# Values on all rows with column halves in turn, scores grouped over row strips, and an output projection that goes token by token: one change to a Trainium2 kernel on one core

## The chip, the cores and the metric

One core of a Trainium2 chip. The metric is the device time of one launch in microseconds; 1990.25 is the median of three runs before the change. Everything is computed in fp32.

## The reference

A hybrid network for 512 tokens of width 1024. Two layers, each: RMS norm, one wide input projection, and from its parts three mixers whose outputs are joined, projected and added to x; then a feed-forward part (norm, up, causal convolution over three tokens, silu gate, down). After a norm, a second block with windowed, grouped-query and cross attention, three gated branches, an output projection with its own norm, and a residual addition. The parts that matter here:

```python
def gla_chunked(q, k, v, log_a):            # 4 heads, keys 32 wide, values 64 wide, chunks of 64 tokens
    ...
        b = jnp.cumsum(gb, axis=-2)
        inter = jnp.einsum('bhik,bhkv->bhiv', qb * jnp.exp(b), state)
        ...
        A = jnp.einsum('bhik,bhjk,bhijk->bhij', qb, kb, dec)
        intra = jnp.einsum('bhij,bhjv->bhiv', A, vb)

def retention_chunked(q, k, v):             # 4 heads of the same sizes, a fixed decay for each head
    ...
    scores = jnp.einsum('bhnid,bhnjd->bhnij', qc, kc) * D[None, :, None]
    intra = jnp.einsum('bhnij,bhnjv->bhniv', scores, vc)
    U = jnp.einsum('bhnjd,bhnjv->nbhdv', k_dec, vc)

# the end of the second block
    merged = gates[:, :, 0] * ya + gates[:, :, 1] * yb + gates[:, :, 2] * ym
    out = merged @ w_out[layer]
    x = x + rms_norm(out, g_post[layer])
```

## The kernel before

**Layout.** x stands in SBUF as eight tiles of 128 channels by 512 tokens (channels on partitions). A dense product in near-fp32 accuracy is three fast matmuls (`mm3`, L442 to 446): both operands are split into a high and a low fp32r part, and high x high, low x high and high x low go into one PSUM bank. `ps` tiles are channel by token (512 tokens moving); `pt` tiles are moved 256 wide. Weights come by DMA in groups (`weight_groups`, L82), three staging buffers, and ACT makes the high and DVE the low part of each (`split_weight`, L411: `whi`, `wlo`; for the output projection `oh`, `ol` in tiles of the general pool).

**Order.** Each engine works in the order in which its instructions stand. Dense projections are generators in a queue (`Fill`, L290). Attention code calls `f(us)` between its small pieces, with a number of the table `PACE` (L28), and the queue then emits dense matmuls worth that time, so that PE has dense work while ACT and DVE prepare the next small piece. `need(name)` empties the queue as far as the named projection.

**The places touched.** `gla` (L774) builds the gated scores by levels: for every level, 32 x 32 to 64 x 64 blocks of decayed keys (`ke`) and queries (`qe`) of four heads are multiplied into four banks `lv`, token tile by token tile, eight instructions (four heads on four 32-row strips, two blocks) and then `f(PACE["gla"])` (L860). DVE copies a level into `gD` under a mask (L871), ACT copies the diagonal blocks from `gD` to `gA` (L875). `states` (L878) makes the chunk states: `U` on PE, then twelve small DVE operations `st`. `mix_out` (L897), which both mixers use, takes two token tiles in one bank `o`: queries times states (L907, `o<-st`), and for each head two value products (L912), one with 64 rows for the first 64 queries, one with 128 rows for the rest; then ACT squares, norm, gate and the transposes `oT`. `ret` (L938) makes its scores head by head: a bank `rsc`, four matmuls on one 32-row strip (L968), DVE's `rA` and dense work. Between `ret`'s scores and its values stands `late()`, the last transposes `yt` of the first mixer (L1056).

PSUM has eight banks: three of tag "d" (`bank`) for dense products and five of tag "m" (`mbank`) in rotation, so that a new tile waits for the readers of the one five before it. `finish` (L1665) does the output projection in two token halves, channel tiles of 128 by 256 tokens; the norm is a sum over channels, which takes PE two small products (`tsq`, `rows`) with DVE's `rsqrt` between, then DVE scales, adds x and SyncE's queue stores; the host transposes the result.

Of the kernel before, what the change touches and what calls it, by code (L numbers as in the profile page):

```python
# [17 lines left out]
S = 512  # L18
# [48 lines left out]
def _span(a, n):  # L67
    return list(range(a, a + n))
# [13 lines left out]
def weight_groups():  # L82
# [69 lines left out]
    two("gm", "w_in_2", k8, _span(GA2 + 1024, 512))  # L152
    branch(1, PAIRED, "w_br_b_2")
    branch(2, k4, "w_br_m_2")
    two("out", "w_out_2", k8, _span(0, 1024))
    return g


# [177 lines left out]
class Prog:  # L336
# [74 lines left out]
    def split_weight(self, i):  # L411
        nc = self.nc
        self.load(i)
        off, k, kt, mc = self.order[i]
        s3 = self.staged.pop(i).rearrange("p (k m) -> p k m", k=kt)
        if i >= self.table[(2, "out", 0)][0]:
            hi, lo = (TileList([self.gt(n, (128, 2, 256), F32R) for _ in range(2)], 2) for n in ("oh", "ol"))
            for j in range(2):
                self.split(hi.tiles[j], lo.tiles[j], s3[:, 2 * j:2 * j + 2])
            self.wt[i] = (k, kt, hi, lo)  # L420
            return
        hi = self.wsp.tile([128, kt, mc], F32R, name="whi", tag="whi")
        lo = self.wsp.tile([128, kt, mc], F32R, name="wlo", tag="wlo")
        nc.scalar.activation(hi, s3, AF.Copy)  # L424
        nc.vector.tensor_sub(lo, s3, hi.bitcast(F32))  # L425
        self.wt[i] = (k, kt, hi, lo)
# [347 lines left out]
    def gla(self, l, bc):  # L774
# [60 lines left out]
        for li, hs in enumerate(seq):  # L835
            qe, ke = nxt
            if li + 1 < len(seq):
                nxt = factors(li + 1, seq[li + 1])
            if li == 1:
                kps = self.mbank("kps")  # L840
                for t in range(3):
                    nc.tensor.transpose(kps[:, T4[t]], kd[:, T4[t]], self.ident)
                kdt = self.gt("kdt")
                nc.scalar.activation(kdt[:, :384], kps[:, :384], AF.Copy)
            if li == 2:
                self.fill.need("gv")
                states = self.states(lambda t: kdt[:, T4[t]], z["gv"], lambda t: eb[:, t * 128 + 127:t * 128 + 128])
            ps = [self.mbank("lv", (128, 4, 64)) for h in range(4)]
            w = hs if hs >= 16 else 64
            step = 2 * hs if hs >= 16 else 64  # L850
            off = hs if hs >= 16 else 0
            for t in range(4):
                for j0 in range(0, 128, step):
                    c0 = (j0 + off) % 64
                    a = t * 128 + j0
                    for h in range(4):
                        hp = slice(32 * h, 32 * h + 32)
                        nc.tensor.matmul(ps[h][j0:j0 + w, t, c0:c0 + w], ke[hp, a:a + w], qe[hp, a + off:a + off + w],  # L858
                                         start=True, stop=True, tile_position=(32 * h, j0))
                f(PACE["gla"])  # L860
            for h in range(4):
                if hs == 64:
                    nc.scalar.activation(A[h][:64, :, 64:], ps[h][:64], AF.Copy)
                elif hs >= 16:
                    for j0 in range(0, 128, step):
                        r, cs = slice(j0, j0 + hs), slice(j0 % 64 + hs, j0 % 64 + 2 * hs)
                        nc.scalar.activation(D[h][r, :, cs], ps[h][r, :, cs], AF.Copy)
                else:
                    mi = MASKED.index(hs)
                    mk = c["gmask"][:, mi * 64:mi * 64 + 64].bitcast(I32)  # L870
                    nc.vector.copy_predicated(D[h], mk[:, None, :].to_broadcast([128, 4, 64]), ps[h])  # L871
            if hs == 0:
                for h in range(4):
                    for r in (slice(0, 64), slice(64, 128)):
                        nc.scalar.activation(A[h][r, :, r], D[h][r], AF.Copy)  # L875
# [21 lines left out]
    def mix_out(self, l, gkey, nkey, A, v, st, qg, bc, b0):  # L897
# [2 lines left out]
        os = []  # L900
        for tp in range(2):
            o = self.mbank("o", (128, 2, 256))
            for j in range(2):
                t = 2 * tp + j
                sl = slice(t * 128, t * 128 + 128)
                if t:
                    nc.tensor.matmul(o[:, j], qg[:, sl], st[t], start=j == 0, stop=True, skip_group_check=True)  # L907
                for h in range(4):
                    hd = slice(64 * h, 64 * h + 64)
                    for n in (64, 128):  # L910
                        r = slice(n - 64, n)
                        nc.tensor.matmul(o[r, j, hd], A[h][:n, t, r], v[t][:n, hd], start=t + h == 0, stop=True,  # L912
                                         skip_group_check=True)
            sq = self.gt("osq")
            nc.scalar.activation(sq, o.rearrange("p t d -> p (t d)"), AF.Square)
            nc.vector.tensor_reduce(v2[:, 8 * tp:8 * tp + 8], sq.rearrange("p (g d) -> p g d", g=8), AX, OP.add)
            os.append(o)
            f(PACE["mix1"])
# [19 lines left out]
    def ret(self, l, bc, late, more):  # L938
# [22 lines left out]
                             c["rqd"][:, None, :].to_broadcast([128, 4, 128]))  # L961
        A = []
        rd = c["rd"].rearrange("p (h i) -> p h i", h=4)
        for h in range(4):
            hp = slice(32 * h, 32 * h + 32)
            ps = self.mbank("rsc", (128, 4, 128))
            for t in range(4):
                nc.tensor.matmul(ps[:, t, :], rk[hp, T4[t]], rq[hp, T4[t]], start=True, stop=True)  # L968
            a = self.gt("rA", (128, 4, 128))
            nc.vector.tensor_mul(a, ps, rd[:, h:h + 1, :].to_broadcast([128, 4, 128]))  # L970
            A.append(a)
            f(PACE["ret2"])
        late()
        for name, g in more:
            self.fill.add(name, g)
# [148 lines left out]
    def run(self):  # L1124
# [9 lines left out]
                if self.stop == (l, "ffn"):  # L1134
                    break
        if self.stop:
            nc.sync.dma_start(self.aps["out"].rearrange("(k p) t -> p k t", p=128), self.x)
            return
        with tc.tile_pool(name="c2", bufs=1) as c2:
            self.cst1 = c2  # L1140
# [2 lines left out]
    def block2(self):  # L1143
# [37 lines left out]
        opm = self.operand("gm", om)  # L1181
        for i in range(4):
            fill.add(("br", 2, i), self.branch(2, i, opm))
        fill.need()
        self.finish()

# [427 lines left out]
    def cross(self):  # L1614
# [47 lines left out]
        self.skew(units, ((0, score), (3, turn), (4, value)), PACE["cross"])  # L1662
        return res

    def finish(self):  # L1665
        nc = self.nc
        for k in range(8):
            self.split(self.xh[:, k], self.xl[:, k], self.merged[k], 0.5)
        kept = {}
        for half in range(2):  # L1670
            tk = slice(256 * half, 256 * half + 256)
            acc = self.gt("acc")[:, :256]
            out = [self.gt("out", (128, 2, 256)) for _ in range(4)]
            for i in range(4):
                if half == 0:
                    kept[i] = list(self.weights((2, "out", i)))
                ps = [self.bank("ps", (128, 256)) for _ in range(2)]
                for k0, kt, hi, lo in kept[i]:
                    for m in range(2):
                        sl = slice(m * 128, m * 128 + 128)  # L1680
                        for k in range(kt):
                            self.mm3(ps[m], hi[:, k, sl], lo[:, k, sl], self.xh[:, k0 + k, tk], self.xl[:, k0 + k, tk],
                                     k0 + k == 0, k0 + k == 7)
                for m in range(2):
                    n = 2 * i + m
                    if n == 0:
                        nc.scalar.activation(acc, ps[m], AF.Square)
                    else:
                        q = self.gt("sq")[:, :256]
                        nc.scalar.activation(q, ps[m], AF.Square)  # L1690
                        nc.vector.tensor_add(acc, acc, q)
                    nc.scalar.activation(out[i][:, m], ps[m], AF.Copy, scale=self.vec("g_post_2", n))
            v = self.tok_sums(acc, 1, 2)
            nc.vector.tensor_scalar(v, v, 1.0 / D, EPS, op0=OP.mult, op1=OP.add)
            r = self.rsqrt(v, "rt", (2, 1))
            R = self.rows(r, 2)[:, :256]
            dst = self.aps["out"].rearrange("(i k p) t -> i p k t", i=4, k=2)
            for i in range(4):
                o = out[i]
                nc.vector.tensor_mul(o, o, R[:, None, :].to_broadcast([128, 2, 256]))  # L1700
                (nc.vector if i else nc.gpsimd).tensor_add(o, o, self.x[:, 2 * i:2 * i + 2, tk])
                nc.sync.dma_start(dst[i][:, :, tk], o)


def arrays_of(inputs):
# [8 lines left out]
    sw = [16 * (d // 16 ^ 1) + d % 16 for d in range(64)]  # L1714
    q, k = inputs["q_norm_2"][0], inputs["k_norm_2"][0]
    a["qkn"] = np.stack([q, q[sw], k, k[sw]])
    a["mla_out"] = np.ascontiguousarray(inputs["mla_out_norm"])
    return a, vec_at, cst_at

# [21 lines left out]
```

## Time and profile before

| | |
|---|---|
| median of three runs | 1990.25 us (1987.42 to 1991.47) |
| profiled execution | 1990.08 us |
| its span | 1988.3 us |
| busy: PE / DVE / ACT / POOL | 98% / 62% / 40% / 7% |
| DMA | 172.30 MB, mean 87 GB/s |

The profile shows one execution. PE is TensorE, DVE VectorE, ACT ScalarE, POOL GpSimd, SP SyncE. Matmuls are pipelined: a dense one shows some 390 ns of duration in the grouped lines (1408 instructions of L444 in 556.8 us), though the next starts earlier; the chain of waits counts from start to start. An fp32 matmul that is not split shows as two records.

### The profile page before, as it was taken

The page shows a single profiled execution, that of the slowest core. Times are in us where ns is not written, and L with a number is a line of the kernel's source. Part 1 is how long each engine was busy: PE and PEld are TensorE (multiplying, and loading weights), DVE is VectorE, ACT ScalarE, POOL GpSimd, SP SyncE. Part 2 cuts the span into 40 slices and gives each one's busy share as a digit, 9 for nine tenths or more (in the row PEclk, how much of TensorE's full clock was granted, in tenths as well). Part 3 has the DMA queues.
Part 4 walks back from the last instruction along what each step waited for, and adds up shares of the span by engine and source line. Part 5 has one row for each costly group of instructions (what it writes and reads, how often), then busy time and mean ns, then how long its engine had stood idle before and what let it go on. Part 6 is the DMA issues. An engine that isn't in the chain of part 4 may idle for free.

```text
span 1988.3 us, 28658 instructions
## 1 busy us (share of the span) xinstructions
PE 1954.8 (98%) x11351; PEld 1620.4 (81%) x11351; DVE 1239.2 (62%) x2299; ACT 793.4 (40%) x1473; POOL 140.7 (7%) x172
## 2 busy tenths in 40 slices
PE   9999999999999999999999999999999999999997
PEld 7879888888888878888888888887888877788887
DVE  6666576646556666576656466845456787655454
ACT  5545243222224635443222224525354456543242
POOL 1000000000000100000000000021131330000000
PEclk9999999999999999999999999999999999999998
DMA  5221123232323321133232334432222221123331
GB/s 196 60 80 44 64 89 101 84 109 85 106 80 107 94 67 50 41 96 95 93 90 96 103 113 123 135 109 67 75 75 67 75 64 54 63 67 98 101 96 54
DMA packets 55189, 172.30 MB, mean 87 GB/s; under 512 B 6494, under 2 KB 10096, under 8 KB 55056
## 3 DMA queue, kind: packets, MB, share of 16 engines
q1 hardware_dynamic: 53152, 165.47, 26.6%
q0 software_dynamic: 1760, 4.87, 0.9%
q8 instruction: 89, 1.46, 0.3%
q14 instruction: 44, 0.36, 0.1%
q10 hardware_dynamic: 144, 0.14, 0.0%
HBM read 167.05 MB, written 2.10 MB: 85 GB/s over the span
## 4 chain that ended last, share of the span: by engine, by line
PE 91%; DVE 5%; ACT 3%; issue 1%; POOL 0%; DMA 0%; DVEq 0%; POOLq 0%; ACTq 0%
PE ps L444 24%; PE ps L446 23%; PE ps L445 23%; PE pt L444 3%; PE pt L445 3%; PE pt L446 3%; PE o L912 2%; DVE wlo L425 1%; PE o L1029 1%; PE s L1006 1%; PE aq L1347 1%; PE bo L1596 1%; PE bpq L1584 1%; PE rows L529 1%; PE lv L858 1%
## 5 line engine op out<-in xcount | busy, mean ns | idle before, releaser
L424 ACT ACTIVATE whi<-wst 128x1024 fp32r<-128x1024 f32 (+3 forms) x318 | 316.3, 995 | 700.3 <-PE ps L445 566.4
L425 DVE TENSOR_TENSOR wlo<-wst,whi 128x1024 fp32r<-128x1024 f32 (+3 forms) x318 | 367.4, 1155 | 315.9 <-ACT whi L424 315.4
L444 PE MATMUL ps<-xh,whi 128*128 128x512 f32 (+1 forms) x1408 | 556.8, 396 | 0.0
L445 PE MATMUL ps<-xl,whi 128*128 128x512 f32 (+1 forms) x1408 | 550.3, 391 | 0.6 <-DVE xl L490 0.6
L446 PE MATMUL ps<-xh,wlo 128*128 128x512 f32 (+1 forms) x1408 | 549.8, 391 | 0.1
L444 PEld LDWEIGHTS ps<-xh,whi 128*128 128x128 f32 (+1 forms) x1408 | 264.4, 188 | 61.1 <-issue 6.7
L446 PEld LDWEIGHTS ps<-xh,wlo 128*128 128x128 f32 (+1 forms) x1408 | 264.3, 188 | 57.1 <-DVE wlo L425 0.9
L445 PEld LDWEIGHTS ps<-xl,whi 128*128 128x128 f32 (+1 forms) x1408 | 264.6, 188 | 55.8 <-DVE xl L490 2.8
L444 PE MATMUL pt<-whi,xh 128*128 128x256 f32 x480 | 143.2, 299 | 1.5 <-ACT bz L1523 0.8
L445 PE MATMUL pt<-wlo,xh 128*128 128x256 f32 x480 | 137.6, 287 | 0.0
L445 PE MATMUL ps<-fl,whi 128*128 128x512 f32 x352 | 137.0, 389 | 0.0
L444 PE MATMUL ps<-fh,whi 128*128 128x512 f32 x352 | 137.0, 389 | 0.0
L446 PE MATMUL ps<-fh,wlo 128*128 128x512 f32 x352 | 136.9, 389 | 0.0
L446 PE MATMUL pt<-whi,xl 128*128 128x256 f32 x480 | 136.5, 286 | 0.0
L444 PEld LDWEIGHTS pt<-whi,xh 128*128 128x128 f32 x480 | 92.7, 194 | 6.7 <-ACT bz L1523 1.3
L1067 DVE TENSOR_TENSOR x<-x,ps 128x512 f32<-128x512 f32 x96 | 65.7, 687 | 50.8 <-PE ps L446 50.6
L445 PEld LDWEIGHTS pt<-wlo,xh 128*128 128x128 f32 x480 | 93.3, 194 | 0.5 <-issue 0.2
L446 PEld LDWEIGHTS pt<-whi,xl 128*128 128x128 f32 x480 | 92.9, 194 | 0.2 <-issue 0.2
L445 PEld LDWEIGHTS ps<-fl,whi 128*128 128x128 f32 x352 | 66.1, 188 | 13.8
L446 PEld LDWEIGHTS ps<-fh,wlo 128*128 128x128 f32 x352 | 66.1, 188 | 13.7
L444 PEld LDWEIGHTS ps<-fh,whi 128*128 128x128 f32 x352 | 66.1, 188 | 13.6
L486 ACT ACTIVATE fh<-cv 128x512 fp32r<-128x512 f32 x44 | 27.9, 633 | 84.7 <-DVE cv L1121 84.7
(464 smaller groups left out, 2919.1 us busy)
## 6 DMA issues: line engine op xcount, KB each, us to landing
wst<-in_w SPq DMA_DIRECT2D x250, 512.0 KB, 3.5
wst<-in_w SPq DMA_DIRECT2D x54, 384.0 KB, 3.0
wst<-in_w SPq DMA_DIRECT2D x20, 256.0 KB, 2.6
x<-in_xT SPq DMA_DIRECT2D x8, 256.0 KB, 4.9
out<-out SPq DMA_DIRECT2D x8, 256.0 KB, 2.3
mt<-in_memT POOLq DMA_DIRECT2D x4, 256.0 KB, 4.1
c<-in_cst POOLq DMA_DIRECT2D x3, 256.0 KB, 3.5
s<-in_cst POOLq DMA_DIRECT2D x3, 256.0 KB, 2.9
```

What stands on the lines that cost most here:

```text
L424: nc.scalar.activation(hi, s3, AF.Copy)
L425: nc.vector.tensor_sub(lo, s3, hi.bitcast(F32))
L444: nc.tensor.matmul(out, lh, rh, start=start, stop=False, skip_group_check=True)
L445: nc.tensor.matmul(out, lh, rl, start=False, stop=False, skip_group_check=True)
L446: nc.tensor.matmul(out, ll, rh, start=False, stop=stop, skip_group_check=True)
L486: nc.scalar.activation(hi, src, AF.Copy)
L529: nc.tensor.matmul(ps[:, t, :], w, self.ident, start=True, stop=True)
L858: nc.tensor.matmul(ps[h][j0:j0 + w, t, c0:c0 + w], ke[hp, a:a + w], qe[hp, a + off:a + off + w], start=True, stop=True, tile_position=(32 ...
L912: nc.tensor.matmul(o[r, j, hd], A[h][:n, t, r], v[t][:n, hd], start=t + h == 0, stop=True, skip_group_check=True)
L1006: nc.tensor.matmul(s[:, :nk], qn[h][:, T4[qt]], kn[h][:, :nk], start=False, stop=True, skip_group_check=True)
L1029: nc.tensor.matmul(O[qt][:, h, :], PT[u][:, T4[kt]], v[kt][:, T4[h]], start=kt == 0, stop=kt == qt)
L1067: nc.vector.tensor_add(xm, xm, ps)
```

## The change

Four edits. In `gla` a level's four token tiles stand in a row, and one pull of four times the pace follows. In `mix_out` the state products of a token pair come first, and every value product uses all 128 rows (the part of `gA` that the mask leaves at zero included), first and second 64 output columns in turn. In `ret` the scores of all heads go to four banks at once, token tile outside and head inside, so that the four 32-row strips take turns, and one pull follows. The output projection keeps tokens on partitions: x is transposed into itself (`residual`, queued between two branches), the split merged activations are the stationary operand, weights move 512 wide in two column groups, the norm is a sum along the free axis (ACT's accumulated square), the gain comes by two broadcasts, and the result is stored without a host transpose.

```diff
@@ weight_groups
-    two("out", "w_out_2", k8, _span(0, 1024))
+    for i in range(2):
+        g.append(((2, "out", i), "w_out_2", 0, k8, _span(512 * i, 512)))
@@ split_weight
-            hi, lo = (TileList([self.gt(n, (128, 2, 256), F32R) for _ in range(2)], 2) for n in ("oh", "ol"))
-            for j in range(2):
-                self.split(hi.tiles[j], lo.tiles[j], s3[:, 2 * j:2 * j + 2])
+            hi, lo = ([self.gt(n, dtype=F32R) for _ in range(kt)] for n in ("oh", "ol"))
+            for j in range(kt):
+                self.split(hi[j], lo[j], s3[:, j])
@@ gla
-                f(PACE["gla"])
+            f(4 * PACE["gla"])
@@ mix_out
             o = self.mbank("o", (128, 2, 256))
+            first = True
             for j in range(2):
                 t = 2 * tp + j
-                sl = slice(t * 128, t * 128 + 128)
                 if t:
-                    nc.tensor.matmul(o[:, j], qg[:, sl], st[t], start=j == 0, stop=True, skip_group_check=True)
+                    nc.tensor.matmul(o[:, j], qg[:, t * 128:t * 128 + 128], st[t], start=first, stop=True,
+                                     skip_group_check=True)
+                    first = False
+            for j in range(2):
+                t = 2 * tp + j
                 for h in range(4):
                     hd = slice(64 * h, 64 * h + 64)
-                    for n in (64, 128):
-                        r = slice(n - 64, n)
-                        nc.tensor.matmul(o[r, j, hd], A[h][:n, t, r], v[t][:n, hd], start=t + h == 0, stop=True,
+                    for r in (slice(0, 64), slice(64, 128)):
+                        nc.tensor.matmul(o[r, j, hd], A[h][:, t, r], v[t][:, hd], start=False, stop=True,
                                          skip_group_check=True)
@@ ret
+        ps = [self.mbank("rsc", (128, 4, 128)) for _ in range(4)]
+        for t in range(4):
+            for h in range(4):
+                hp = slice(32 * h, 32 * h + 32)
+                nc.tensor.matmul(ps[h][:, t, :], rk[hp, T4[t]], rq[hp, T4[t]], start=True, stop=True)
         for h in range(4):
...
-            f(PACE["ret2"])
+        f(4 * PACE["ret2"])
@@ block2
         for i in range(4):
             fill.add(("br", 2, i), self.branch(2, i, opm))
+            if i == 1:
+                fill.add("res", self.residual())
@@ new function
+    def residual(self):
+        nc = self.nc
+        self.xt = self.x.rearrange("p (a b) s -> p a (b s)", b=2).rearrange("p a (t c) -> p a t c", t=4)
+        for kp in range(4):
+            ps = [self.mbank("xT", (128, 2, 2, 128)) for _ in range(2)]
+            for t in range(4):
+                for b in range(2):
+                    nc.tensor.transpose(ps[t // 2][:, t % 2, b], self.x[:, 2 * kp + b, self.T4[t]], self.ident)
+            for j in range(2):
+                nc.scalar.activation(self.xt[:, kp, 2 * j:2 * j + 2], ps[j].rearrange("p t b c -> p t (b c)"), AF.Copy)
+            yield 0.9
@@ finish, the part behind the split of merged (the old body is left out)
+        ss = self.small("oss", (4, 2))
+        y = {}
+        def ev(t, c, ps):
+            sq = self.gt("osq2")
+            nc.scalar.activation(sq, ps, AF.Square, accum_out=ss[:, t, c:c + 1])
+            y[t, c] = self.gt("oy2")
+            nc.vector.tensor_mul(y[t, c], ps, g[c])
+        ps = [self.bank("ps") for _ in range(3)] + [self.mbank("po")]
+        for k0, kt, hi, lo in self.weights((2, "out", 0)):
+            for k in range(kt):
+                for t in range(4):
+                    self.mm3(ps[t], self.xh[:, k0 + k, T4[t]], self.xl[:, k0 + k, T4[t]], hi[k], lo[k],
+                             k0 + k == 0, k0 + k == 7)
+        for t in range(4):
+            ev(t, 0, ps[t])
+        kept = list(self.weights((2, "out", 1)))
+        for t in range(4):
+            ps = self.mbank("po")
+            for k0, kt, hi, lo in kept:
...
+            ev(t, 1, ps)
+            v = self.small("ov", (1,))
+            nc.vector.tensor_reduce(v, ss[:, t], AX, OP.add)
...
+            for c in (1, 0):
+                o = y[t, c].rearrange("p (a b) -> p a b", a=2)
+                nc.vector.scalar_tensor_tensor(o, o, r, self.xt[:, 2 * c:2 * c + 2, t], op0=OP.mult, op1=OP.add)
+                (nc.sync if c else nc.scalar).dma_start(self.aps["out"][T4[t], 512 * c:512 * c + 512], y[t, c])
```

The order of the instructions on PE, for the gated scores of the first layer near their end (`lv` the score banks, `gq`, `gk`, `qe`, `ke` queries and keys; `ps` a dense projection). Before:

```order
L858 MATMUL lv<-qe_419,ke_421 64x64 x8
L444 MATMUL ps<-cqh,whi 128x512
L445 MATMUL ps<-cql,whi 128x512
L446 MATMUL ps<-cqh,wlo 128x512
L858 MATMUL lv<-qe_419,ke_421 64x64 x8
L444 MATMUL ps<-cqh,whi 128x512
```

and after the change:

```order
L447 MATMUL ps<-cqh,wlo 128x512
L859 MATMUL lv<-gq,gk 64x64 x32
L445 MATMUL ps<-cqh,whi 128x512
L446 MATMUL ps<-cql,whi 128x512
L447 MATMUL ps<-cqh,wlo 128x512
```

Four bursts of eight became one of 32, and the dense matmuls that stood between them follow it in one piece (21 of them here).

PE between the decayed scores and values of the first layer (`U` the states' products, `rsc` the scores, `yt` the transposes of `late()`, `pt` a dense projection). Before, the scores stood as 4, 8 and 4 with dense pieces between, and these are the last four:

```order
L446 MATMUL pt<-whi,xl 128x256
L968 MATMUL rsc<-rT 128x128 x4
L1056 MATMUL yt<-c_ident,on 128x128 x4
L912 MATMUL o<-tv,rA 64x64
L444 MATMUL pt<-whi,xh 128x256
```

After the change, from the dense matmuls ahead of U:

```order
L445 MATMUL pt<-whi,xh 128x256
L446 MATMUL pt<-wlo,xh 128x256
L447 MATMUL pt<-whi,xl 128x256
L887 MATMUL U<-tv,rkd 32x64 x12
L972 MATMUL rsc<-rT 128x128 x16
```

and, behind twelve dense matmuls that follow rsc,

```order
L445 MATMUL pt<-whi,xh 128x256
L446 MATMUL pt<-wlo,xh 128x256
L447 MATMUL pt<-whi,xl 128x256
L1061 MATMUL yt<-c_ident,on 128x128 x4
L908 MATMUL o<-st,qd 128x256
```

So yt stands 12 dense matmuls behind U, where 36 dense matmuls and all scores were between.

ACT in `finish` after the change (`oh` high parts of the output weights, `osq` squares of the first column group's four banks):

```order
L487 ACTIVATE oh<-wst 128x512 x3
L1699 ACTIVATE osq_16810,oss<-ps 128x512
L1699 ACTIVATE osq_16814,oss<-ps 128x512
L1699 ACTIVATE osq_16818,oss<-ps 128x512
L1699 ACTIVATE osq_16822,oss<-po 128x512
L487 ACTIVATE oh<-wst 128x512 x6
L1699 ACTIVATE osq_16879,oss<-po 128x512
```

Six of the second group's eight high parts stand behind the four squares of the first group.

## Rows read from the trace of the kernel before

**Rows 1.** The page: busy time by engine, and the chain that ended last by engine.

```profile
PE 1954.8 (98%) x11351; PEld 1620.4 (81%) x11351; DVE 1239.2 (62%) x2299; ACT 793.4 (40%) x1473; POOL 140.7 (7%) x172
...
PE 91%; DVE 5%; ACT 3%; issue 1%; POOL 0%; DMA 0%; DVEq 0%; POOLq 0%; ACTq 0%
```

**Rows 2.** Chain of waits, decayed part of layer one: start us, us, what.

```profile
199.55 0.47 PE U L886 x24
200.02 1.08 PE rsc L968 x8
...
202.73 1.64 PE rsc L968 x16
...
207.44 1.08 PE rsc L968 x8
...
217.06 0.43 PE o L907 x2
...
222.65 0.23 PE ps L445
...
229.02 0.23 PE ps L446
229.25 0.87 PE oT L933 x8
```

**Rows 3.** Windows, all engines: stretch, length, busy time and records, PE clock, DMA.

```profile
687.00:691.00 4.00, 4.00 (x23) 4.00 (x23) 2.05 (x3) 1.87 (x4) 0.58 (x1) 0.57 0.33 90
701.00:704.50 3.50, 3.50 (x33) 3.16 (x30) 2.37 (x5) 1.58 (x5) 0.00 (x0) 0.51 0.29 80
...
1927.20:1951.40 24.20, 24.20 (x201) 23.97 (x200) 13.00 (x24) 12.52 (x29) 0.00 (x0) 1.00 0.30 89
```

**Rows 4.** Chain of waits, gated scores and values of layer one.

```profile
104.00 0.30 PE lv L858 x16
104.30 0.43 PE ps L444
...
120.98 1.06 ACT whi L424
122.04 0.28 ACT gA L863
...
128.62 2.05 PE o L912 x16
```

**Rows 5.** Windows of the four mix_outs, tile o alone: the sum.

```profile
sum 60.90, PE 41.15 PEld 27.96 DVE 0.00 ACT 2.47; mean PE 10.29 PEld 6.99 DVE 0.00 ACT 0.62
```

**Rows 6.** Chain of waits at a unit of the window attention.

```profile
1357.85 1.02 PE ao L1363 x16
```

**Rows 7.** Timeline of PE at a merged level: start us, us, engine, line, operation.

```profile
79.06 0.86 PE L858 MATMUL lv<-qe,ke 32*64 32x64 f32 x58
79.85 0.39 PE L444 MATMUL pt<-whi,xh 128*128 128x256 f32 x1
```

**Rows 8.** Timeline of DVE behind U in the decayed part of layer one.

```profile
201.17 2.44 DVE L893 SCALAR_TENSOR_TENSOR st<-st,c_rdec,U 32x64 f32<-32x64 f32 x8
203.64 1.29 DVE L970 TENSOR_TENSOR rA<-rsc,c_rd 128x512 f32<-128x512 f32 x2
```

**Rows 9.** Chain of waits, end of the program.

```profile
1974.73 0.13 PE ps L446
1974.89 0.39 ACT sq L1690
...
1976.78 0.18 DVE ss L1694
...
1978.75 0.17 DVE rt L500
...
1984.18 0.69 DVE out L1701
```

**Rows 10.** Waits of PE: engine, tile, whom it waited for; us, times, longest.

```profile
PE rows L529 <- DVE Rqt L500: 4.0, 2, 2.0
```

More of the change, by code (lines that the diff above doesn't have):

```diff
@@ L963, in ret @@
         rd = c["rd"].rearrange("p (h i) -> p h i", h=4)
+        ps = [self.mbank("rsc", (128, 4, 128)) for _ in range(4)]
[3 more added lines that the diff above has]
+                nc.tensor.matmul(ps[h][:, t, :], rk[hp, T4[t]], rq[hp, T4[t]], start=True, stop=True)
         for h in range(4):
[L965 to L968, printed above, removed]
             a = self.gt("rA", (128, 4, 128))
-            nc.vector.tensor_mul(a, ps, rd[:, h:h + 1, :].to_broadcast([128, 4, 128]))
+            nc.vector.tensor_mul(a, ps[h], rd[:, h:h + 1, :].to_broadcast([128, 4, 128]))
             A.append(a)
-            f(PACE["ret2"])
+        f(4 * PACE["ret2"])
         late()
@@ L1136, in run @@
         if self.stop:
-            nc.sync.dma_start(self.aps["out"].rearrange("(k p) t -> p k t", p=128), self.x)
+            nc.sync.dma_start(self.aps["out"].rearrange("t (k p) -> p k t", p=128), self.x)
             return
@@ L1663, in cross @@
         return res
-    def finish(self):
-        nc = self.nc
+    def residual(self):
[9 more added lines that the diff above has]
+            yield 0.9
@@ L1667, in finish @@
+    def finish(self):
+        nc, T4 = self.nc, self.T4
+        g = []
+        for c in range(2):
+            t = self.gt("gpost")
+            src = self.aps["gpost"]
+            nc.gpsimd.dma_start(t, bass.AP(tensor=src.tensor, offset=src.offset + 512 * c, ap=[[0, 128], [1, 512]]))
+            g.append(t)
         for k in range(8):
             self.split(self.xh[:, k], self.xl[:, k], self.merged[k], 0.5)
[L1669 to L1693, printed above, removed]
-            nc.vector.tensor_scalar(v, v, 1.0 / D, EPS, op0=OP.mult, op1=OP.add)
[L1695 to L1702, printed above, removed]
@@ new lines, in finish @@
+        for t in range(4):
[4 more added lines that the diff above has]
+            for k0, kt, hi, lo in kept:
+                for k in range(kt):
+                    self.mm3(ps, self.xh[:, k0 + k, T4[t]], self.xl[:, k0 + k, T4[t]], hi[k], lo[k],
+                             k0 + k == 0, k0 + k == 7)
+            ev(t, 1, ps)
+            v = self.small("ov", (1,))
+            nc.vector.tensor_reduce(v, ss[:, t], AX, OP.add)
+            nc.vector.tensor_scalar(v, v, 1.0 / D, EPS, op0=OP.mult, op1=OP.add)
+            r = self.rsqrt(v, "ort", (1,))
+            for c in (1, 0):
+                o = y[t, c].rearrange("p (a b) -> p a b", a=2)
+                nc.vector.scalar_tensor_tensor(o, o, r, self.xt[:, 2 * c:2 * c + 2, t], op0=OP.mult, op1=OP.add)
+                (nc.sync if c else nc.scalar).dma_start(self.aps["out"][T4[t], 512 * c:512 * c + 512], y[t, c])
@@ L1716, in arrays_of @@
     a["qkn"] = np.stack([q, q[sw], k, k[sw]])
+    a["gpost"] = np.ascontiguousarray(inputs["g_post_2"])
     a["mla_out"] = np.ascontiguousarray(inputs["mla_out_norm"])
@@ L1735 @@
         aps[name] = nc.dram_tensor(f"in_{name}", a.shape, F32, kind="ExternalInput").ap()
-    aps["out"] = nc.dram_tensor("out_0", (D, S), F32, kind="ExternalOutput").ap()
+    aps["out"] = nc.dram_tensor("out_0", (S, D), F32, kind="ExternalOutput").ap()
     with tile.TileContext(nc) as tc:
@@ L1739 @@
     r = run_bass_kernel_spmd(nc, [{f"in_{k}": v for k, v in arrays.items()}], core_ids=[0])
-    return np.ascontiguousarray(r.results[0]["out_0"].T)[None]
+    return np.ascontiguousarray(r.results[0]["out_0"])[None]
```

## The prediction

> **What bounds the kernel now.** I read the page first: its busy shares and its chain say which engine to count in [rows 1]. TensorE (PE) is busy 98% of the span and 91% of the chain that ended last; VectorE (DVE) has 5% of it, ScalarE (ACT) 3%. So a microsecond saved on PE is a microsecond of the kernel, unless PE then runs into a wait. The profiled execution took 1990.08 us (span 1988.3), 0.2 us under the median of 1990.25; all sums go against it.
>
> Then I read the chain of waits where the change lies, since it lists PE from start to start while the grouped lines count overlapping durations. Dense matmuls of 512 columns go at (229.02 - 222.65) / 28 = 0.2275 us, those of 256 columns at 24.20 / 201 = 0.120 [rows 2, 3]. Each small burst between them costs its own time and delays the first dense matmul behind it: 0.43 us where its neighbours take 0.23, so 0.20 for coming back [rows 4].
>
> **Values and state products (mix_out).** PE spends 41.15 us on tile o in the four mix_outs (two layers, gated and decayed) [rows 5], 10.3 each. The chain shows why: eight value instructions (16 records; every fp32 instruction is two) take 2.05 us, 0.256 each [rows 4]. Half of them use 64 of the array's rows and half 128, by turns, and they do not overlap. After the change all 16 of a token pair use 128 rows with the two 64-column halves in turn. The window attention already does exactly that: ao (128 x 64 weights, halves in turn) runs 16 records of 128 columns in 1.02 us, 0.064 each [rows 6]. Ours move 64 columns, so I take half of it, 0.032: 32 records x 0.032 = 1.02 us for a token pair. The row that speaks for less is U, 128 rows with column quarters in turn, 24 records in 0.47, 0.0196 for 32 weight columns [rows 2]; doubled for 64 columns it gives 0.039, 1.25 us a pair. If nothing shrinks with the columns, 0.064 stays and a pair is 2.05. I take the ao figure, which has the same weights. The state products are untouched at 0.43 for two [rows 2]: now grouped, they no longer cost the 0.2 of a change of form between each. A mix_out becomes 2 x 1.02 values, 0.65 for three state products and some 1.35 to enter and leave the bursts: 4.05, against 10.3 and its own return delays, 10.6 together. Saved: 4 x 6.55 = **26.2 us**; by 1.25 a pair 24.4, by 2.05 a pair 18.
>
> The Trainium skill, "TensorE: Matmul & The Clock Gate", Part 3 "What overlaps and what doesn't", says that a weight load overlaps running matmuls only if its row group differs. That would forbid what I count on, for all values now share all rows; what it would make of the sum is worked out as the first rival. The ao rows speak against it: all of them use all 128 rows and still come every 0.064 us [rows 6].
>
> **Gated scores (gla).** By the order, the last levels of a layer stand in 21 bursts, most of eight instructions, a dense stretch after each. One costs 0.30 us [rows 4] and 0.20 for coming back: about 0.50, so 10.4 for a layer. Four token tiles now follow one another: 6 bursts remain, of 32, 32, 2, 30, 32 and 16 instructions. Such a merged run is in the trace already: 58 records in 0.79 us (79.06 to 79.85), 0.0136 each [rows 7]. So 64 records are 0.87 + 0.20 = 1.07, and the six sum to 5.3 with the two small ones at 0.45 and 0.64. Saved: 5.2 a layer, **10.4 us**.
>
> **Decayed scores (ret).** Per layer the chain has 1.08, 1.64 and 1.08 us for rsc (eight records, sixteen, eight) and two return delays [rows 2]: four matmuls in a row share one 32-row strip and do not overlap, 1.08 / 8 = 0.135 a record. Sixteen in turn over four strips I put at 1.0: 32 records of 128 columns, where two halves in turn took 0.064 a record [rows 6], so four strips half of that. 3.8 + 0.4 - 1.0 - 0.2 = 3.0; two layers **6.0 us**. If strips in turn do not overlap, nothing but a delay is saved, 2 x 0.2.
>
> **What PE meets when it comes early.** In the gated part the chain leaves PE just before the values: it runs through ACT's whi 120.98 and the last gA 122.04 to the values at 122.36 [rows 4]. PE has no lead to spare there, and the change brings it 5.2 us forward. DVE's masked copies and ACT's gA also start earlier, since their scores do, but not the query rotation between them, whose PSUM bank PE needs again for the dense stretch. Ends: nothing, or the whole 5.2; I take half, 2.75 a layer, **+5.5 us**. Before the decayed values, DVE's state updates end at 203.61, 3.6 us after U ended at 200.02 [rows 2, 8]. The token transposes yt take over U's PSUM bank, so they wait for those updates; PE arrives after rsc (1.0) and 12 short dense matmuls (1.44 + 0.2), 2.6 us after U: 1.0 lost. The four score multiplications (rA, two in 1.29 us) start only then and hold the values 0.65 more; the final oT loses some 0.4, since the values end sooner than the normalisation can. Ends: nothing, or 3.0 (all that the scores gain there); I take 2.05 a layer, **+4.1 us**.
>
> **The end (finish).** 384 matmuls of 256 columns with the first half's norm between them, 1927.2 to 1974.86, are 47.7 us [rows 3, 9]; 192 of 512 columns are 43.7. Moved on ACT: six of the eight high parts of the second column group now stand behind four squares, and DVE's low parts behind four gain products; PE has two k-tiles to work on meanwhile, and I add 0.8. -3.2. The tail behind the last matmul is 1988.3 - 1974.86 = 13.4 us, with two trips to PE (tsq and rows) and eight wide DVE operations [rows 9]. Afterwards the last token tile has a square of twice the width (2 x 0.39), a reduce and eleven small DVE operations (eleven fill 1976.78 to 1978.93 now; with one more, 2.35), two wide ones at 0.69, and from the last one to the end 3.43 as now: 7.9 to 8.0. -5.4. Against it PE gets 32 transposes of x, of the form of oT (eight in 0.87 us [rows 2]): +3.6 with the entry. Their eight ACT copies lie beside dense work of PE and cost nothing there; without that cover they would cost some 8 x 0.69, the price of a wide DVE operation. The two broadcasts on GpSimd's queue and the last DMAs' second queue cost nothing, queued behind nothing late. Together **-5.0 us**.
>
> **The clock.** The two new waits may let the granted clock fall. Stretches at 1.2 GHz are there: the mean is 0.57 for 687 to 691 and 0.51 for 701 to 704.5, which loses (1 - 0.57) x 4.0 = 1.7 us and as much again [rows 3]. PE's longest waits for norm rows (Rqt), 2.0 us in each layer [rows 10], are of the size of the new ones. I add one stretch and a bit, **+2**.
>
> **Sum.** -26.2 - 10.4 - 6.0 + 5.5 + 4.1 - 5.0 + 2 = -36.0; 1990.1 - 36.0 = **1954.1 us**. With its own terms at their nearer ends (values 24.4, half of the waits more or less) the forecast reaches from 1948 to 1961.
>
> **Rivals.**
> - Weight loads bound the packed values. At 0.064 a record whatever the columns, 18 is saved instead of 26.2: 1962. With no overlap at all a record costs what rsc's now does, 0.135 [rows 2], less 0.054 for the 64 columns that it lacks (oT, 128 columns: 0.87 / 8 = 0.109): 0.081, 2.6 a pair, 13.6 saved: 1967. The latter is what the rule cited above would give. For it: the changed tiles move only 64 columns for each load. Against: U at 0.0196. Chance 0.09.
> - PE's waits take back more, because DVE and ACT set the pace of gla and ret once PE is short there: their upper ends, 10.4 and 6.0 instead of 5.5 and 4.1, and two more low stretches: 1964. For it: the chain through ACT at 122 [rows 4]. Against: over the whole span they are far from busy. Chance 0.10.
> - No waits: the copies follow the scores at once, and the yt bank is free in time. 1954.1 - 9.6 - 2 = 1942.5. Against: 203.61. Chance 0.07.
> - Slower: the clock. PE's new waits lie in every layer's gated and decayed part, 122 to 222 us in the first [rows 2, 4]. If the granted clock fell at the first and stayed at 1.2 GHz to the end of the decayed values, 100 us of work in each layer would take twice as long, +200: some 2150. It decides from 36 us of full-speed work done at half the clock, about 21 stretches such as the two in the rows. Against it: both ended within 4 us although dense work was as broken there [rows 3]. Chance 0.02. The Trainium skill, same page, Part 4, adds that transposes do not count as busy work for the clock in the same way, which would put the 32 new ones under it as well; no row here has so many in a run.
> - The change does not do what it says: the order shows the bursts merged, so 0.01 for an unchanged time.
>
> **How the numbers follow.** The forecast has 0.71. The range takes in the ends of its terms and the rivals of 1964 and 1962: 1943 to 1966. 0.2% is 4 us, about what a measurement can tell from no change; only the last two rivals come near it. Faster 0.96, within 0.02, slower 0.02.
>
> **What would show it.** Right: tile o at some 15 us of PE for the four mix_outs in place of 41.15; lv bursts as one row of the timeline; rsc at 1.0; a wait before yt of about 1 us, behind DVE's st; a wait in front of the gated values; a tail of 8 us. Wrong: values at 0.06 us a record or more, waits of over 5 us a layer in the gated part, or PE's clock at half for tens of us.

## The result, and the profile after

Four runs of the changed kernel took 1957.72 us in the median (1955.74 to 1961.33), four of the kernel before, on the same chip, 1989.45. The ratio is 0.9843, with a 95% interval of 0.9824 to 0.9861: some 31 us less, where 36.0 were forecast (1954.1 us, range 1943 to 1966). The profiled execution took 1958.88 us, its span is 1957.1, 31.2 less than before.

The page, busy time and the chain by engine, beside [rows 1]:

```profile
PE 1922.7 (98%) x11179; PEld 1593.6 (81%) x11179; DVE 1234.4 (63%) x2311; ACT 788.8 (40%) x1465; POOL 141.4 (7%) x172
...
PE 89%; DVE 6%; ACT 3%; issue 1%; POOL 1%; DMA 0%; SPq 0%; DVEq 0%; ACTq 0%
```

PE is still the engine to count on, but two points of its chain went to DVE and GpSimd. The windows of the four mix_outs, tile o alone, beside the 41.15 of [rows 5]:

```profile
sum 57.10, PE 16.69 PEld 13.10 DVE 0.00 ACT 4.76; mean PE 4.17 PEld 3.28 DVE 0.00 ACT 1.19
```

24.5 us of PE are gone. Here is PE's timeline in the gated part of the first layer (start us, us, engine, line, operation, records, and in brackets the idle time before and who ended it), against [rows 4, 7]:

```profile
105.21 0.91 PE L859 MATMUL lv<-gq,gk 32*64 32x64 f32 x64
...
114.50 0.59 PE L908 MATMUL o<-st,qg 128*128 128x256 f32 x2
118.53 0.76 PE L445 MATMUL ps<-ckh,whi 128*128 128x512 f32 x1 [3.44 <-DVE rt L769]
```

A level of four token tiles is one row of 64 records now. There is also a new wait: PE stands still for 3.44 us until DVE's `rt` frees the PSUM bank of the query rotation. PE's waits in the whole span (us in total, times, longest) show it once in each layer, and with it the waits at yt and at the values:

```profile
PE ps L445 <- DVE rt L769: 6.9, 2, 3.4
...
PE yt L1061 <- DVE st L894: 2.3, 2, 1.1
...
PE o L908 <- DVE rA L975: 0.3, 2, 0.2
```

What DVE did meanwhile, by its timeline:

```profile
112.60 1.22 DVE L426 TENSOR_TENSOR wlo<-wst,whi 128x1024 fp32r<-128x1024 f32 x1
115.66 1.41 DVE L763 TENSOR_TENSOR qr<-qt,qr 64x512 fp32r<-64x512 f32 x2 [1.84 <-ACT qr L762]
117.09 0.69 DVE L768 TENSOR_TENSOR sw<-ps,s 128x512 f32<-128x512 f32 x1
117.70 0.68 DVE L769 TENSOR_TENSOR rt<-ps,c 128x512 f32<-128x512 f32 x1
```

DVE takes its work in order: `qr` of the first half waits for ACT, which waits for GpSimd's addition `qt`; `sw` and `rt` of the second half, whose input has long been in PSUM, stand behind it. ACT's and GpSimd's timelines have the two steps ahead of `qr`:

```profile
115.00 1.28 ACT L762 ACTIVATE qr<-qt 64x512 fp32r<-64x512 f32 x2 [2.43 <-POOL qt L773]
```

```profile
112.65 2.32 POOL L773 TENSOR_TENSOR qt<-rt,sw 128x512 f32<-128x512 f32 x1 [36.83 <-ACT whi L425]
```

These are the values and state products of the decayed part, by the chain (start us, us, what); [rows 4] have 2.05 us for 16 value records:

```profile
201.12 1.08 PE o L916 x32
...
205.34 0.86 PE o L908 x4
206.20 1.08 PE o L916 x32
```

The end of the program, PE's last row from its timeline and then the chain:

```profile
1948.25 0.39 PE L447 MATMUL po<-oh,xl 128*128 128x512 f32 x1
```

```profile
1948.81 0.70 ACT osq L1699 x2
...
1952.43 0.75 DVE oy L1725
```

The last matmul ends at 1948.64. From there to the end at 1957.1 are 8.5 us, against 13.4 before.

### The profile page after: what moved, and what is told of

Its sections match the earlier page's. It is cut to its first block, busy times and chain, and to the rows that moved or that the text cites. A ratio compares the mean times of both kernels' runs of the same rounds, so it can differ in the third digit from the quotient of the medians.

```text
span 1957.1 us, 28290 instructions
## 1 busy us (share of the span) xinstructions
PE 1922.7 (98%) x11179; PEld 1593.6 (81%) x11179; DVE 1234.4 (63%) x2311; ACT 788.8 (40%) x1465; POOL 141.4 (7%) x172
## 4 chain that ended last, share of the span: by engine, by line
PE 89%; DVE 6%; ACT 3%; issue 1%; POOL 1%; DMA 0%; SPq 0%; DVEq 0%; ACTq 0%
PE ps L445 23%; PE ps L447 23%; PE ps L446 23%; PE pt L445 3%; PE pt L447 3%; PE pt L446 3%; PE o L1034 1%; PE s L1011 1%; DVE wlo L426 1%; PE aq L1354 1%; PE bo L1603 1%; PE bpq L1591 1%; ACT whi L425 1%; PE rows L530 1%; DVE st L894 0%
```

## The experiments

All times are device times, medians with the range in brackets; ratios are to the kernel before on the same chip, with a 95% interval. The median of the kernel before was 1988.9 us on the chip of the first four, 1992.28 on that of the next four and 1989.21 on that of the last three. Three stages are named by PE's tiles: `yt`, the transposes of the first mixer in `late()`; `cf`, the transposes of the factors with which the window attention's parts are combined, and `cw`, the products behind it; `bs`, the scores of the grouped-query attention.

**One part at a time, on the kernel before.** Each carries one of the four edits of the diff above, without the others.

Values and state products (the edit in `mix_out`):

> Values alone on the kernel before. Theory (the forecast's first term, with the waits only where PE comes early): the four mix_outs save 26 us, PE reaches the gated values no earlier than before, so no wait there; 1 us goes at oT. 1989 - 25 = 1964 us, tile o about 15 us of PE. Rival (weight loads bound the packed values): a burst of 32 records takes 2 us or more, 1971 to 1976 us. Rival (the waits of the whole change come from the faster values): waits of 3 us a layer appear here too, 1970 us.

Measured: 1967.62 us (1966.23 to 1969.45), ratio 0.9901 [0.9885, 0.9918]. A whole burst in its timeline, and behind cf a window (stretch, length, busy time of PE, PEld, DVE, ACT, POOL, PE's clock, DMA share, GB/s):

```profile
128.69 1.15 PE L915 MATMUL o<-tv,gA 128*64 128x64 f32 x32
```

```profile
1557.00:1569.00 12.00, 11.65 (x32) 7.11 (x33) 6.88 (x13) 2.69 (x4) 5.62 (x5) 0.57 0.17 44
```

No wait on rt and none at gA is among PE's waits, so the waits don't come from fast values alone. The profiled span, 1964.7, is 23.6 us shorter than before, although it has 10 us at half the clock (1.2 of 2.4 GHz) behind cf, where the kernel before had none. So most of the theory's 25 is there, and the clock took some of it back.

Gated scores:

```diff
-                f(PACE["gla"])
+            f(4 * PACE["gla"])
```

> Only the regrouped gated scores on the kernel before. Theory: bursts save 5.1 us a layer and the wait on DVE's rotation (rt) gives 3.4 back, so 3.4 us in all: 1986 us, with a PE wait before the ps of the query rotation of about 3.4 us a layer. Rival (the wait comes from the other edits, not from this one): no such wait, 1979 us. Rival (it also drags the granted clock down for 3.4 us behind each wait): 1989 us, no gain.

Measured: 1999.1 us (1991.16 to 2002.8, ten runs), ratio 1.0045 [1.0031, 1.0059]: slower than before, more than the worst rival. PE's wait and two windows:

```profile
PE ps L444 <- DVE rt L768: 7.3, 2, 3.6
```

```profile
119.00:123.00 4.00, 3.26 (x9) 2.18 (x10) 2.34 (x4) 1.27 (x2) 2.15 (x1) 0.57 0.21 24
734.00:755.00 21.00, 19.74 (x70) 13.66 (x71) 8.31 (x13) 4.18 (x6) 2.71 (x2) 0.52 0.12 37
```

The wait is there in full, 3.6 us a layer, and behind it the granted clock is at half: 3 us in the first layer, 20 us in the second. The values of the old form follow in both, so they alone don't set the length. The ten runs had mean clocks of 0.983 to 0.989, the kernel before 0.992 to 0.996, and the slowest were those with the lowest clock. The profiled run, 1992.55, is the second fastest of the ten; where the others were slow no trace shows.

Decayed scores (the edit in `ret`):

> Only the regrouped decayed scores on the kernel before. Theory: the scores save 3.0 us a layer, the wait of yt for DVE's state updates (1.1) and for rA (0.2) gives 1.3 back: 3.4 us in all, 1986 us. Rival (row strips in turn do not overlap): no gain, the wait costs, 1990 us or more. Rival (yt's wait comes only with fast values): 1983 us.

Measured: 1985.04 us (1979.43 to 1990.41, ten runs), ratio 0.9984 [0.9971, 0.9996]. The time can't tell the theory (1986) from the last rival (1983), but the waits speak for that rival: yt does not wait. In PE's timeline 4.4 us of dense work stand between the scores and yt, 36 matmuls, where the whole change has 12:

```profile
199.43 0.39 PE L444 MATMUL pt<-whi,xh 128*128 128x256 f32 x1
...
203.84 0.60 PE L1057 MATMUL yt<-c_ident,on 128*128 128x128 f32 x4
```

The end (`finish`, `residual`, and what they need):

> Only the output projection token by token, with the residual's transposes, on the kernel before. Theory: 8.7 us less from the first output matmul to the end, 3.4 us more for 32 transposes: 1989 - 5.3 = 1984 us. Rival (the transposes or their copies cost more than their time on PE): 1987 us or more. The granted clock in the stretch of the attention's combination (cf, cw) should be as in the kernel before, since nothing ahead of it is changed.

Measured: 1983.6 us (1980.54 to 1990.58, ten runs), ratio 0.9979 [0.9968, 0.9989]: 5.3 us by the medians, as forecast, 4.2 by the ratio. Its clock has no low stretch behind cf, as expected.

By the medians the four alone make -21.3 + 10.2 - 3.9 - 5.3 = -20.3 us, the whole change -31.7: one part is bad alone, and less so with the others.

**The wait taken away.** One edit, in `uq_dense`: the low parts that wait for GpSimd and ACT are issued 4 us of dense work later, so that DVE reads the second half first.

```diff
             self.rope64(t, ps, CR, SR)
-            self.stack(qr[2 * m:2 * m + 2], t)
+            self.fill.after(4.0, lambda: self.stack(qr[2 * m:2 * m + 2], t))
```

On the changed kernel:

> The changed kernel with one edit: the two halves of the query rotation are both read out of PSUM (sw, rt) before DVE does the first half's low part (qr), which waits for GpSimd and ACT. Theory (DVE stands still in front of qr, and rt of the second half behind it holds PE's bank for 3.4 us a layer; the clock then falls for 3.4 us each time, 1.7 lost): both go, 2 x (3.4 + 1.7) = 10 us less, 1948 us, no PE wait on rt. Rival (another wait follows at once, the values for gA): 1953 to 1956 us with a wait on gA of 2 us or so. Rival (the bank is not what PE waits for): no change, 1958 us.

Measured: 1943.51 us (1941.93 to 1948.08), ratio 0.9768 [0.9746, 0.979]. That beats both kernels: by the medians 14 us less than the changed one in its first set of runs, 10 less than in its second (at the end of this section), and the ratio's interval lies apart from both. PE's waits no longer have rt, none at gA took its place, and the windows where it stood show full work at full clock:

```profile
112.00:128.00 16.00, 15.96 (x125) 12.74 (x126) 14.76 (x31) 9.58 (x16) 3.95 (x3) 1.00 0.46 146
712.00:728.00 16.00, 15.94 (x140) 13.35 (x140) 14.68 (x29) 7.98 (x11) 1.78 (x2) 1.00 0.36 116
```

The same edit on the kernel before, with the gated scores regrouped and no other part of the change:

> The kernel before with the regrouped gated scores and the query rotation's second half read before qr. Theory (regrouping alone came out slower by its wait on rt and the low clock that follows it): without the wait it gives its 5.1 us a layer, 1979 us. Rival (the regrouping loses for another reason): 1990 us or more.

Measured: 1977.92 us (1974.71 to 1980.48), ratio 0.9936 [0.9913, 0.996]. The regrouping that lost 10 us alone gains some 13 with this edit (1992.28 x 0.0064, 8 to 17 by the interval): the loss was the wait and what followed it, not the grouping. The edit without the regrouping was not run; the kernel before has no wait on rt that it could take away.

**The other waits.** The pull of dense work ahead of cf, on the changed kernel:

```diff
-    com3=3.0,
+    com3=5.2,
```

> The changed kernel with the pull ahead of the combination's transposes (cf) raised from 3.0 to 5.2 us, so that PE has dense work while DVE makes cF. Theory (the 2.1 us wait at cf starts the 27 us at half the clock in the changed kernel's profile): wait and stretch go, half of 27 less what the later wait of bs took up before (3.9 and half of 6.8): 4 to 6 us less, 1952 to 1954 us, PE clock 1.00 through cw. Rival (the stretch is set off by the small cw matmuls themselves): the wait goes but the low clock stays, 1956 us. Rival (dense work only moves, bs waits longer): 1958 us.

Measured: 1957.39 us (1955.48 to 1959.02), ratio 0.9834 [0.9813, 0.9854], as the changed kernel. The wait hardly moved:

```profile
PE bs L1578 <- DVE bqT L763: 4.1, 1, 4.1
...
PE cf L1432 <- DVE cF L1428: 1.7, 1, 1.7
```

```profile
1552.00:1579.00 27.00, 27.00 (x116) 18.64 (x115) 23.65 (x26) 7.83 (x12) 18.23 (x12) 1.00 0.20 64
```

The wait remains nearly whole (1.7 of 2.1), and bs waits too; the low clock behind cf was not there, although the wait was. So this run doesn't tell whether the wait sets it off, and the edit is worth nothing.

All three together, the yt transposes (`late()`) moved ahead of U:

```diff
         f(PACE["ret1"])
+        late()
         st = self.states(lambda t: kd[:, T4[t]], z["rv"], lambda t: c["rdec"])
...
         f(4 * PACE["ret2"])
-        late()
```

> The changed kernel with three edits: the query rotation's second half read before qr, the last token transposes (yt) moved ahead of U so that they do not take U's bank, and the longer pull ahead of cf. Theory (the waits and the clock behind them are what is left): 10 for the first, 2 x 1.1 for the second, 5 for the third: 1940 us. Rival (each wait is replaced by the next one on the same chain): 1950 us or more.

Measured: 1946.98 us (1945.44 to 1950.0), ratio 0.9787 [0.9762, 0.9811]: no better than the rotation's edit alone (1943.51). The waits behind U changed names:

```profile
PE o L916 <- DVE rA L976: 1.1, 4, 0.3
PE o L908 <- DVE st L894: 1.0, 2, 0.5
...
PE rsc L973 <- DVE yal L488: 0.9, 2, 0.4
```

They are 3.0 us, in place of the 2.3 at yt and 0.3 at the values. There the rival was right: three waits on DVE replace the two, whatever PE does ahead of them.

**Which overlap is worth what.** Both on the version with the rotation read early (v1_stack). Values with the first column half for all heads, then the second:

```diff
-                for h in range(4):
-                    hd = slice(64 * h, 64 * h + 64)
-                    for r in (slice(0, 64), slice(64, 128)):
+                for r in (slice(0, 64), slice(64, 128)):
+                    for h in range(4):
+                        hd = slice(64 * h, 64 * h + 64)
```

> The version with the rotation read early (1943.5 us), but the value products take the first 64-column half for all four heads and then the second, so that neighbours share a column half. Theory (the gain needs the halves in turn, since only then two products run side by side): a burst of 32 records goes from 1.08 us to about 2.6 (0.081 a record, the price without overlap), 8 bursts, 12 us more: 1956 us. Rival (most of the gain is that all tiles have the same 128-row form, whatever their order): bursts stay near 1.1 to 1.4 us, 1943 to 1946 us.

Measured: 1951.14 us (1944.54 to 1951.67), ratio 0.9809 [0.9792, 0.9825]. The chain, first of this kernel and then of the version with the halves in turn:

```profile
116.66 1.47 PE o L916 x32
```

```profile
118.42 1.08 PE o L916 x32
```

That is 0.39 us a burst and 3.1 us for the eight bursts, far less than 12. In mechanism the rival has it: tiles of one form take 1.47 us even with neighbours on one half, where the mixed forms take 2.05 for half as many records. The median went up by more than 3.1, to neither forecast. The one profiled run, 1944.54 us, has a mean clock of 0.996 and the three others, 7 us slower, have 0.991; the clock is the likely reason, but none of the three was profiled.

The decayed scores head by head, grouping kept (the two loops exchanged):

> The same version, but the sixteen decayed scores go head by head (one 32-row strip four times, then the next) instead of strips in turn; the grouping stays. Theory (strips in turn overlap): rsc takes 16 x 0.27 = 4.3 us instead of about 1.1, 3.2 more a layer, of which the 1.1 us wait of yt takes back its own: 2 x 2.1 = 4 us more, 1948 us, and no wait of yt. Rival (the wait of yt is not for U's bank and does not shrink): 1950 us. Rival (strips overlap in any order): 1943.5 us.

Measured: 1942.33 us (1940.54 to 1943.69), ratio 0.9763 [0.9748, 0.9777]: no slower than 1943.51. PE's timeline, first strips in series, then (rotation's version) in turn:

```profile
189.19 2.82 PE L972 MATMUL rsc<-rT 32*128 32x128 f32 x32
193.48 0.60 PE L1061 MATMUL yt<-c_ident,on 128*128 128x128 f32 x4
```

```profile
189.27 1.18 PE L972 MATMUL rsc<-rT 32*128 32x128 f32 x32
193.19 0.66 PE L1061 MATMUL yt<-c_ident,on 128*128 128x128 f32 x4 [1.13 <-DVE st L894]
```

Strips in turn do save 1.64 us of PE, and PE then waits 1.13 at yt (and 0.16 behind it): most of it is handed back to DVE's state updates. The order of the strips gains nothing here that the runs can show, so the time is that of the last rival, but not for its reason. The series took 2.82 us, not the 4.3 expected: 0.09 a record, where short bursts of eight had 0.135 [rows 2].

**The changed kernel once more:**

> The changed kernel once more, unchanged. Theory (the 27 us at half the clock behind cf in its profile is not a property of the program alone but falls differently from run to run): this profile has another length there, and the times spread over some 6 us as before, 1955 to 1961 us. Rival (the stretch belongs to the program): again 27 us at the same place.

Measured: 1953.67 us (1952.42 to 1954.46), ratio 0.982 [0.9805, 0.9834]. The same window in the first profile and in this one, and this one's wait ahead of it:

```profile
1552.00:1579.00 27.00, 27.00 (x59) 16.16 (x58) 16.40 (x21) 5.64 (x9) 15.22 (x12) 0.50 0.09 30
```

```profile
1552.00:1579.00 27.00, 26.71 (x120) 18.92 (x120) 24.46 (x29) 9.23 (x14) 18.59 (x12) 1.00 0.24 70
```

```profile
PE cf L1432 <- DVE cF L1428: 2.1, 1, 2.1
```

The clock is at half in one and full in the other, with the same instructions and the same 2.1 us wait at cf ahead, and in the same time PE gets through 59 records at half and 120 at full. The stretch doesn't belong to the program. Of the other eleven traces, all with a wait of 1.7 to 2.1 us there, p5_gla_stack's has a low stretch just as long behind cf, two have shorter ones and eight have none. This is p5_gla_stack's:

```profile
1568.00:1596.00 28.00, 28.00 (x63) 16.91 (x62) 17.63 (x22) 5.66 (x9) 16.45 (x12) 0.51 0.09 32
```

Instead this profile shows 0.52 from 117 to 124 us and 0.54 from 718 to 725, behind the two waits on rt, each longer than in the first.

## Why the prediction was right, point by point

- **Values, -26.2.** PE lost 24.5 us on tile o, and the edit alone gave 21.3 in time. A burst is 1.08 us against the forecast 1.02 and the 1.25 from U. The size was right; the reason given was half right. I credited it to column halves running side by side, by the row of ao; the exchange of loops shows that the equal form of all tiles does most of it (2 x 2.05 to 1.47 us) and the turn the smaller part (1.47 to 1.08). That the weights share all row groups did not hinder it: at 0.034 us a record the first rival is out, and so is the rule of the Trainium skill ("TensorE: Matmul & The Clock Gate", Part 3) for these tiles. The Trainium skill, "TensorEngine Tiling (Array Packing)", Key Properties, says that a change of tiling mode drains the engine. The 1.47 with one form against 4.1 with two forms agree with it.
- **Gated scores, -10.4.** 64 records take 0.91 us in the timeline with their own tail, 1.07 with the return was forecast; with the wait out of the way the regrouping is worth some 13 us, and the interval of 8 to 17 takes in the forecast.
- **Its wait, +5.5.** It came at the place and for the reason named (the query rotation's bank), 6.9 us for both layers. What I did not see is how narrow the cause is: one in-order queue in which `qr` stands ahead of `rt`. One line takes it away.
- **Decayed scores, -6.0, and their wait, +4.1.** Alone, without a wait, the edit gave 3.9 us (1 to 6 by the interval); in the whole change yt waits 1.13 a layer and o 0.16, 2.6 in all, so the wait was put too high. What is left of the two in the whole change no run shows by itself. The reason for the gain was half right: I read 0.135 a record as the price of one strip without overlap, but the 3.8 us of the bursts fall to 2.82 in one series and to 1.18 with strips in turn, so part of the gain is fewer bursts, and most of the turn's part is handed back to DVE.
- **The end, -5.0.** 5.3 alone. The stall of 0.8 for the second column group didn't come: from the first output matmul at 1904.81 to the end of the last are 43.8 us, and 43.7 were counted without it. The tail is 8.5 instead of 8.0.
- **The clock, +2.** This is the term that was mis-sized. At the first cw of the attention's combination, before the end is reached, the traces are 32.0 us apart, as the terms ahead of it make it (26.2 + 10.4 + 6.0 - 5.5 - 4.1 = 33.0). Low stretches of 3.4 us do stand behind the two new waits on rt, but two that the kernel before had [rows 3] are gone (stretch, length, PE's busy time, clock, DMA share, GB/s):

```profile
118.00:122.00 4.00, 3.47 (x24) 0.57 0.18 53
718.00:723.00 5.00, 4.17 (x39) 0.66 0.24 77
```

  The timelines of PE, before and after:

```profile
1584.93 0.73 PE L1433 MATMUL cw<-cfr,selr 16*128 16x512 f32 x4
...
1618.47 0.63 PE L1571 MATMUL bs<-bkh,bqT 128*128 128x512 f32 x1
```

```profile
1552.89 1.22 PE L1440 MATMUL cw<-cfr,selr 16*128 16x512 f32 x4
...
1592.07 0.47 PE L1578 MATMUL bs<-bkh,bqT 128*128 128x512 f32 x1
```

  33.5 us on in the kernel before they are 26.4 apart. The changed kernel's run was at half the clock for 27 us between the two; the one before was there for 7 us and waited 3.9 us for bs, a wait that the slow stretch covers in the other:

```profile
1612.00:1620.00 8.00, 5.96 (x16) 0.57 0.21 66
```

```profile
PE bs L1571 <- DVE bqT L762: 3.9, 1, 3.9
```

  26.4 and the 4.8 us by which the rest is shorter make the 31.2 between the spans. In the second set of runs, whose profile has no such stretch, the kernel took 1953.67, next to the 1954.1 of the forecast. That closeness is partly luck: there the stretches behind rt were twice as long, and the misses of the other terms have either sign (values 1.7 too much saved, the wait on rt 1.4 too little, those at yt and the values 1.5 too much).
- **The rivals.** The one that gave more waits (1964) had 16.4 us of them, the forecast 9.6, and 6.9 + 2.3 + 0.3 = 9.5 came; only its longer low clock did. The one that gave none (1942.5) is close to the 1943.51 of the version that reads the rotation early, but the wait at yt remains there, so the equal number is chance. The slower one, by the clock, names what p2's edit did alone, where regrouped scores with the old values lost 10 us to the wait and the clock behind it. The 32 transposes, which it put under the clock too, ran at full clock, by their window:

```profile
1868.00:1873.00 5.00, 5.00 (x40) 1.00 0.18 45
```

What stays open: what sets off the low stretch behind cf in some runs and not in others, and why it lasts 27 us in one and is missing in another. The runs show that neither the instructions nor the wait alone decide it.

## What to carry to other kernels

Where an engine is 98% busy, a faster piece of it can move the bound to the next in-order queue: look for what stands behind a waiting instruction there although its own input is ready, and let the reader of a PSUM bank go ahead of it. Give small products one tile form in a row first (4.1 to 1.47 us here) and let column halves take turns second (to 1.08). Try each part of a joint change alone and look at the granted clock behind every new wait, since the loss there can be larger than the wait.

## What the runs showed of the hardware that was not expected

GpSimd's addition of 128 x 512 took 1.28 us in the kernel before and 2.32 in the changed one, with the same operands. In the changed kernel DVE's `wlo` (two operands from SBUF) ran beside it from 112.60; in the version with the rotation read early the first addition (beside DVE reading PSUM) takes 1.30 and the second, beside `wlo`, 2.10. GpSimd's timelines, of the kernel before and then of that version:

```profile
114.88 1.28 POOL L772 TENSOR_TENSOR qt<-rt,sw 128x512 f32<-128x512 f32 x1 [38.98 <-DVE sw L769]
```

```profile
112.91 1.30 POOL L773 TENSOR_TENSOR qt<-rt,sw 128x512 f32<-128x512 f32 x1 [36.85 <-ACT whi L425]
114.73 2.10 POOL L773 TENSOR_TENSOR qt<-rt,sw 128x512 f32<-128x512 f32 x1 [0.53 <-PE ps L446]
```

The Trainium skill, "SBUF — State Buffer", Who interferes with whom, says that a DVE instruction with two SBUF inputs contends with a GpSimd instruction that reads SBUF, and that the one that starts first blocks the other. These durations agree with it. Since `qr` and with it `rt` wait for the addition, about one microsecond of the 3.44 us wait is that, by the timelines; no run took it out alone.

The other was the size of what follows a wait: behind 3.6 us without work on PE the clock was at half for 20 us in one layer and for 3 in the other of the same run (p2_gla).
